# A row of silu(c) and a gate row leave the pool of load buffers: six shared places become four and two

## The chip, the cores and the metric

The kernel runs on one core of one Trainium2 chip. The time is device microseconds (us) of one execution. Before the change it was run three times: the median is 1897.98 us, the lowest 1897.97 and the highest 1900.49. One more execution was profiled; it took 1898.33 us, and its span, from the first to the last instruction in the trace, is 1896.6 us.

## What is computed

One residual block over 256 tokens of width 2048, in float32. Three sublayers follow each other, each with its own shift, scale and gate, which all come from one vector c:

```python
mod = (jax.nn.silu(c) @ w_ada[l] + b_ada[l]).reshape(B, N_SUBLAYERS, 3, D_MODEL)
shift, scale, gate = mod[:, :, 0], mod[:, :, 1], mod[:, :, 2]
y = _swiglu(modulate(x, 0), ffn1_w13[l], ffn1_w2[l])
x = _layer_norm(ALPHA * x + FFN_WEIGHT * gate[:, 0, None, :] * y, ln_g[l, 0], ln_b[l, 0])
u = modulate(x, 1)
...
y = jnp.concatenate([h_m, h_r], axis=-1) @ w_out[l]
x = _layer_norm(ALPHA * x + gate[:, 1, None, :] * y, ln_g[l, 1], ln_b[l, 1])
y = _swiglu(modulate(x, 2), ffn2_w13[l], ffn2_w2[l])
x = _layer_norm(ALPHA * x + FFN_WEIGHT * gate[:, 2, None, :] * y, ln_g[l, 2], ln_b[l, 2])
```

The first and the last sublayer are feed-forward networks (FFN) with an inner width of 5632; the middle one is the mixer, which runs four mLSTM heads beside a gated linear recurrence.

## The kernel before

**Weights.** All weights are read once, as tiles of 128x2048 floats (1 MB). Such a tile is loaded into a "raw" buffer by the SP queue (`load`, line 96, or `load_w`, line 115) and then split in two by `split` (line 103): ScalarE (ACT) rounds it into a "hi" tile (line 110) and VectorE (DVE) writes the rest into a "lo" tile (line 112). There are three hi and three lo buffers. The raw buffer is free again when the lo tile is written. TensorE (PE) then makes three products, hi by hi, lo by hi and hi by lo, so a tile in the FFNs is 24 matmuls of 512 columns.

**The raw pool.** `raw_tile` (line 84) hands out one of six equal places of 128x2048 floats (`RAW`, line 46). Not only weights live there. The row of silu(c), copied to all partitions (`scb`, line 171), takes one at the start and keeps it until its last reader. The gate of a sublayer (`gate`, line 191) takes another: `gate_rows` (line 224) writes the gate to HBM and reads it back to all partitions (line 233), and for the second and third sublayer it takes a new raw tile for that first (line 232). Beside these, rows of the layer norms (`ln_rows`, line 263), the recurrence's weights `wax` (line 1240) and the tile `sums` (line 690) pass through.

**The ada tiles.** The product of silu(c) with w_ada is made on DVE: 144 tiles are loaded into raw places, and each is multiplied with `scb` and summed by one instruction (line 209). `tick` (line 217) hands them out at a rate per load: 0.88 in the first FFN, 0.5 in the mixer and in the last FFN (lines 40 to 42). The last 16 of them, the third gate, fall into the first blocks of the last FFN.

**The last FFN.** After two ordinary blocks (`rows_block`, line 668), the blocks 2 to 9 are `fast_block` (line 710), which computes a 2x2 block product with seven products in place of eight. Of its loads, the tile `ta` (line 748) lives long: it is changed in place by subtractions at lines 755 and 760 and is read for the last time at line 774. `tc_` (line 752) is changed at line 765 and read until line 766, `td` (line 758) until 765. Each block has 12 loads: `ta`, `tc_`, `td`, `tb` (line 769), g2 and g3, two v tiles, and four of w2 (`x_tile`, line 732). Then follow a half block, `gate_rows` for the third gate, and `closing` (line 1025), which loads twelve w2 tiles, three of them multiplied with the gate (line 1034), and then the last layer norm's two rows.

**What sets the order.** Most instructions aren't ordered by hand. The framework orders the queue of each engine when the program is built (`schedule_with_timeline_sim`, line 1554): it goes through the instructions by their order in the code, with times of its own for each, and where the next one isn't ready in its reckoning (no place free, no data yet) it puts a later one first. On the chip each queue then runs in that fixed order. So a load is issued when it is at the head of SP's queue and its place is free, and an instruction on DVE or ACT that waits holds up all behind it. Instructions issued through `V`, `A`, `G`, `T` (line 140) keep the order of the code among themselves.

Of the kernel before, what the change touches and what calls it, by code (L numbers as in the profile page):

```python
# [11 lines left out]
F32 = mybir.dt.float32  # L12
# [4 lines left out]
P = 128  # L17
D = 2048
# [24 lines left out]

SLOT = 2176

RAW = 6

FAST = range(2, 10)


# [10 lines left out]
def block_kernel(ctx: ExitStack, tc: tile.TileContext, a: dict, out: bass.AP):  # L61
    nc = tc.nc
    cst = ctx.enter_context(tc.tile_pool(name="cst", bufs=1))
    big = ctx.enter_context(tc.tile_pool(name="big", bufs=1))
    wp = ctx.enter_context(tc.tile_pool(name="wp", bufs=1))
# [4 lines left out]
    def slot(name, dtype=F32):  # L70

        return ph.tile([P, SLOT], dtype, tag="slot", bufs=6, name=name)
# [5 lines left out]
    def bank(name):  # L78
        return psp.tile([P, 512], F32, tag="ps", name=name)
# [4 lines left out]
    def raw_tile(name):  # L84
        n_raw[0] += wide[0]
        if wide[0] and n_raw[0] % 3 == 0:
            return slot(name)[:, 0:D]
        return wp.tile([P, 2048], F32, tag="raw", bufs=RAW, name=name)


    credit = [0.0, 0.0]
# [1 line left out]

    fine = [False]

    def load(src, name, into=None):

        tick()
        raw = raw_tile("r" + name)
        queue().dma_start(raw, src)  # L100
        return raw, name, into

    def split(tile, act, low):

        raw, name, into = tile
        hi, lo = into() if into else [wp.tile([P, 2048], F32R, tag=w, bufs=3, name=w[0] + name) for w in ("hi", "lo")]
        step = 512 if fine[0] else 2048
        cols = [slice(c, c + step) for c in range(0, 2048, step)]
        for w in cols:
            act.copy(cut(hi, w), like(raw[:, w], hi))  # L110
        for w in cols:
            low.tensor_sub(cut(lo, w), like(raw[:, w], lo), cut(hi, w).bitcast(F32))  # L112
        return hi, lo

    def load_w(src, name, into=None):

        return split(load(src, name, into), nc.scalar, nc.vector)
# [24 lines left out]
    def queue():  # L142

        return Q if wide[0] else nc.sync
# [23 lines left out]
            T.matmul(ps[:, 0:P], ident, ident, start=True, stop=True)  # L168


    scb = raw_tile("scb")
    sc = cst.tile([P, KT], F32, name="sc")
    nc.scalar.dma_start(sc, a["c"])
    nc.scalar.activation(sc, sc, AF.Silu)
# [13 lines left out]
    badac = cst.tile([P, 3, 3, KT], F32, name="badac")  # L188
    adac = cst.tile([P, 3, 3, KT], F32, name="adac")
    modc = adac[:, :, 0:2, :]  # L190
    gate = Held(raw_tile("gate0"))
    dr = ctx.enter_context(tc.tile_pool(name="dr", bufs=1, space=bass.MemoryType.DRAM))
    rowd = dr.tile([KT, P], F32, name="rowd")
    xd = dr.tile([P, NT, D], F32, name="xd")
# [22 lines left out]
    def tick():  # L217

        credit[0] += credit[1]
        while todo and credit[0] >= 1.0:  # L220
            credit[0] -= 1.0
            ada_tile(V if wide[0] else nc.vector)

    def gate_rows(s, weight):

        ps = bank(f"adag{s}")
        nc.tensor.transpose(ps[0:KT, 0:P], adac[:, s, 2, :], ident)
        row = sm.tile([KT, P], F32, tag="grow", bufs=1, name=f"grow{s}")
        nc.scalar.mul(row, ps[0:KT, 0:P], weight)
        nc.gpsimd.dma_start(rowd, row)  # L230
        if s:
            gate.tile = raw_tile(f"gate{s}")
        nc.gpsimd.dma_start(gate[:, :], rowd.rearrange("a b -> (a b)").rearrange("(o n) -> o n", o=1).to_broadcast([P, D]))


# [48 lines left out]
    def mov_t(ps, hl, acth, actl, k0, t, first, last, pe=nc.tensor, **kw):  # L284

        hi, lo = hl
        tk = slice(t * P, (t + 1) * P)
        for j in range(4):
            w = slice(j * 512, (j + 1) * 512)
            o = like(ps, hi)  # L290
            pe.matmul(o, acth[:, k0 + j, tk], cut(hi, w), start=first and j == 0, stop=False, **kw)  # L291
            pe.matmul(o, acth[:, k0 + j, tk], cut(lo, w), start=False, stop=False, **kw)  # L292
            end = pe.matmul(o, actl[:, k0 + j, tk], cut(hi, w), start=False, stop=last and j == 3, **kw)  # L293
        return end
# [21 lines left out]
    def mov_w(pss, hl, acth, actl, k0, first, last, pe=nc.tensor):  # L316
        for t in range(NT):
            end = mov_t(pss[t], hl, acth, actl, k0, t, first, last, pe)
        return end
# [333 lines left out]
    def ffn(s, w13, w2, start, following=None):  # L653
# [11 lines left out]
        def new_h(gi):  # L665
            hts[gi] = [slot(f"{w}{gi}", F32R)[:, 0:GRP * S].rearrange("p (a b) -> p a b", a=GRP) for w in ("hth", "htl")]
# [43 lines left out]
        def fast_block(b, wh, wl):  # L710

            i = 8 * b
            gi = 4 * b // GRP - 1
            s2_, s4_, s3_, s1_ = 0, 4, 8, 12
            p1, p5 = bank(f"fa{b}"), bank(f"fb{b}")
            py = {}

            def part(ps, hl, h, k0, t, first, last):
                return mov_t(ps, hl, *h, k0, t, first, last, T, skip_group_check=not first and ps in (p1, p5))

            def fresh(k):
                return load(w13[i + k], f"fw{s}_{b}{k}")

            def halves(tile, w=""):
                return split((tile[0], tile[1] + w, None), nc.scalar, nc.vector)

            def kept(ps, tag, w):
                to = sm.tile([P, 512], F32, tag=tag, bufs=2, name=f"{w}{s}{b}")
                nc.scalar.copy(to, ps)
                return to  # L730

            def x_tile(m):
                n, k = b % 2 * 2 + m // 2, m % 2
                if not k:
                    py[n] = [bank(f"py{gi}_{n}_{t}") for t in range(NT)]
                kg = 2 * gi + k
                end = mov_w(py[n], load_w(w2[kg * 4 + n], f"w2{s}_{kg}_{n}"), *hts[gi], k * 4, not k, k == 1, T)
                if k:
                    c = slice(n * 512, (n + 1) * 512)
                    for t in range(NT):  # L740
                        if gi == 0:
                            evac.append(nc.scalar.copy(yacc[t][:, c], py[n][t]))
                        else:
                            nc.vector.tensor_add(yacc[t][:, c], yacc[t][:, c], py[n][t])
                return end

            u, w = (uh, ul), (wh, wl)
            ta = fresh(0)
            end = part(p1, halves(ta), u, 0, 0, True, True)
            turn_one(end)  # L750
            f1 = kept(p1, "u", "fs")
            tc_ = fresh(4)
            end = x_tile(0)
            turn_one(end)
            nc.vector.tensor_sub(ta[0], tc_[0], ta[0])
            part(p5, halves(ta, "p"), w, s1_, 0, True, True)
            f5 = kept(p5, "gy", "ft")
            td = fresh(5)
            x_tile(1)
            nc.vector.tensor_sub(ta[0], td[0], ta[0])  # L760
            part(p1, halves(ta, "q"), w, s2_, 0, False, True)
            f2 = kept(p1, "gy", "fv")
            part(p5, halves(td), w, s4_, 0, False, False)
            x_tile(2)
            nc.vector.tensor_sub(tc_[0], td[0], tc_[0])
            part(p1, halves(tc_, "q"), w, s3_, 0, False, True)
            f3 = kept(p1, "u", "fu")
            p2, p4 = bank(f"fc{b}"), bank(f"fd{b}")
            tb = fresh(1)
            part(p2, halves(tb), u, 4, 0, True, False)  # L770
            g2_ = load_w(w13[i + 2], f"fw{s}_{b}2")
            part(p2, g2_, u, 8, 0, False, False)
            part(p4, g2_, u, 8, 1, True, False)
            nc.vector.tensor_sub(tb[0], tb[0], ta[0])
            part(p4, halves(tb, "p"), u, 4, 1, False, False)
            g3_ = load_w(w13[i + 3], f"fw{s}_{b}3")
            part(p2, g3_, u, 12, 0, False, True)
            part(p4, g3_, u, 12, 1, False, True)
            nc.vector.tensor_add(f1, f1, p2)
            nc.scalar.activation(f1, f1, AF.Silu)  # L780
            nc.vector.tensor_add(f3, f3, p4)
            nc.scalar.activation(f3, f3, AF.Silu)
            x_tile(3)
            vs = [load_w(w13[i + 4 + k], f"fw{s}_{b}{4 + k}") for k in (2, 3)]
            for t, ps in enumerate((p5, p1)):
                for k in range(2):
                    part(ps, vs[k], u, 8 + 4 * k, t, False, k == 1)
            if 4 * b // GRP not in hts:
                new_h(4 * b // GRP)
            for t, h, v, ps in ((0, f1, f2, p5), (1, f3, f5, p1)):  # L790
                nc.vector.tensor_add(v, v, ps)
                nc.vector.tensor_mul(h, h, v)
                to_turn.append((b, t, h))
# [341 lines left out]
    def mixer(following):  # L1135
# [151 lines left out]
        rg_out()  # L1287
        ada_until(1, 2, KT - 1)
        gate_rows(1, 1.0)


# [266 lines left out]
```

## Time and profile before

| | value |
|---|---|
| median of three runs | 1897.98 us |
| profiled execution | 1898.33 us |
| its span | 1896.6 us |
| PE busy | 1864.0 us (98%) |
| DVE busy | 1562.4 us (82%) |
| ACT busy | 895.8 us (47%) |
| HBM read | 514.46 MB, 273 GB/s over the span |
| silu(c)'s row read last, from | 1377.3 us |
| stages, roughly | first FFN to 770 us, mixer to 1168, last FFN to the end |

The span is 1.7 us shorter than the profiled execution's time. PE stands for matmuls, and its busy time is the union of them; a matmul of 512 columns is listed with some 390 ns, but as they are pipelined one starts every 0.227 us when nothing is missing. "Idle before" in a row is the time for which the engine stood still ahead of it, with what ended the wait. SPq rows are the loads' issues.

### The profile page before, as it was taken

What the parts mean: (1) busy time and instruction counts of PE and PEld (TensorE: products, weight loads), DVE (VectorE), ACT (ScalarE), POOL (GpSimd) and SP (SyncE); (2) the same over time, 40 slices, a digit from 0 to 9 for tenths busy, and PEclk for the clock granted to TensorE, in tenths of its full rate; (3) what the DMA queues carried; (4) which work ended last, traced back from release to release, by engine and by line L of the source; (5) the groups of instructions that cost most, each with busy time, mean ns of one, the idle gap of its engine ahead of it and who ended that gap; (6) DMA issues with size and microseconds to landing.
All of it is one profiled execution on the core that took longest, in us unless ns stands there. A gap on an engine that the chain in (4) does not pass through costs nothing.

```text
span 1896.6 us, 21239 instructions
## 1 busy us (share of the span) xinstructions
PE 1864.0 (98%) x8495; PEld 1527.8 (81%) x8495; DVE 1562.4 (82%) x1467; ACT 895.8 (47%) x847; POOL 41.0 (2%) x68
## 2 busy tenths in 40 slices
PE   8999999999999999999699999999999999999998
PEld 5788888888888888788588887887788888888886
DVE  6899998887887977898976777798987788778776
ACT  4533444534333334756534346645555454555441
POOL 0000000000000000000000021000000000000000
PEclk9999999999999999999899999999999999999999
DMA  9999889989999886586487666758765654565661
GB/s 351 417 364 357 319 313 362 349 342 350 352 358 353 336 329 246 195 298 228 159 329 288 223 221 214 297 222 333 270 233 206 222 200 164 212 223 208 236 222 67
DMA packets 74931, 520.06 MB, mean 274 GB/s; under 512 B 8736, under 2 KB 8912, under 8 KB 13520
## 3 DMA queue, kind: packets, MB, share of 16 engines
q1 hardware_dynamic: 72144, 507.54, 71.0%
q0 software_dynamic: 960, 7.37, 1.0%
q10 hardware_dynamic: 1728, 3.80, 0.6%
q8 instruction: 66, 1.08, 0.2%
q14 instruction: 33, 0.27, 0.0%
HBM read 514.46 MB, written 4.22 MB: 273 GB/s over the span
## 4 chain that ended last, share of the span: by engine, by line
PE 92%; DVE 4%; ACT 2%; DMA 1%; issue 1%; POOL 0%; POOLq 0%; DVEq 0%; ACTq 0%
PE py L135 9%; PE pj L280 5%; PE fa L135 5%; PE fb L135 4%; PE fd L135 3%; PE fc L135 3%; PE py L292 3%; PE py L291 3%; PE py L293 3%; PE pj L282 3%; PE fg L292 3%; PE fg L293 3%; PE fg L291 3%; PE fv L293 2%; PE fv L291 2%; PE fv L292 2%
## 5 line engine op out<-in xcount | busy, mean ns | idle before, releaser
L209 DVE CUSTOM_DVE_ANT_0 ada<-ada,scb,badac 128x2048 f32<-128x2048 f32 x110 | 257.9, 2345 | 21.7 <-DMA ada<-in_w_ada 21.7
L110 ACT CAST hw<-rw 128x2048 fp32r<-128x2048 f32 x81 | 155.1, 1914 | 215.9 <-DMA rw<-in_w 51.0
L112 DVE TENSOR_TENSOR lw<-rw,hw 128x2048 fp32r<-128x2048 f32 x81 | 185.2, 2288 | 63.1 <-ACT hw L110 62.3
L112 DVE TENSOR_TENSOR lfw<-rfw,hfw 128x2048 fp32r<-128x2048 f32 x56 | 128.2, 2290 | 28.3 <-ACT hfw L110 28.1
L110 ACT CAST hfw<-rfw 128x2048 fp32r<-128x2048 f32 x56 | 107.3, 1915 | 58.6 <-PE py L135 28.2
L280 PE MATMUL pj<-u,hs 128*128 128x512 f32 x512 | 122.5, 391 | 0.0
L110 ACT CAST hra<-rra 128x2048 fp32r<-128x2048 f32 x38 | 72.6, 1914 | 101.7 <-DMA rra<-in_w_r 46.3
L280 PEld LDWEIGHTS pj<-u,hs 128*128 128x128 f32 x512 | 94.3, 188 | 18.4
L110 ACT CAST hs<-rs 128x2048 fp32r<-128x2048 f32 x32 | 61.1, 1909 | 83.9 <-PE pj L280 69.0
L135 PE MATMUL py<-lw,hth 128*128 128x512 f32 x256 | 99.7, 389 | 0.8 <-DVE lw L112 0.8
L135 PE MATMUL py<-hw,hth 128*128 128x512 f32 x256 | 100.4, 392 | 0.0
L292 PE MATMUL py<-lw,hth 128*128 128x512 f32 x256 | 99.9, 390 | 0.1
L135 PE MATMUL py<-hw,htl 128*128 128x512 f32 x256 | 99.7, 389 | 0.0
L293 PE MATMUL py<-hw,htl 128*128 128x512 f32 x256 | 99.7, 389 | 0.0
L291 PE MATMUL py<-hw,hth 128*128 128x512 f32 x256 | 97.3, 392 | 0.0
L110 ACT CAST hfg<-rfg 128x2048 fp32r<-128x2048 f32 x28 | 53.6, 1915 | 82.4 <-DMA rfg<-in_w 51.6
L112 DVE TENSOR_TENSOR lfv<-rfv,hfv 128x2048 fp32r<-128x2048 f32 x28 | 64.1, 2289 | 30.5 <-ACT hfv L110 30.2
L292 PE MATMUL fg<-lfg,u 128*128 128x512 f32 x224 | 87.4, 390 | 0.1
L293 PE MATMUL fg<-hfg,u 128*128 128x512 f32 x224 | 87.3, 390 | 0.0
L292 PE MATMUL fv<-lfv,u 128*128 128x512 f32 x224 | 87.2, 389 | 0.0
L293 PE MATMUL fv<-hfv,u 128*128 128x512 f32 x224 | 87.1, 389 | 0.0
L112 DVE TENSOR_TENSOR ls<-rs,hs 128x2048 fp32r<-128x2048 f32 x32 | 73.1, 2283 | 17.0 <-ACT hs L110 17.0
(723 smaller groups left out, 4733.1 us busy)
## 6 DMA issues: line engine op xcount, KB each, us to landing
ada<-in_w_ada SPq DMA_DIRECT2D x138, 1024.0 KB, 6.3
rw<-in_w SPq DMA_DIRECT2D x81, 1024.0 KB, 5.4
rfw<-in_w SPq DMA_DIRECT2D x64, 1024.0 KB, 4.8
rra<-in_w_r SPq DMA_DIRECT2D x45, 1024.0 KB, 7.0
rs<-in_w_s SPq DMA_DIRECT2D x32, 1024.0 KB, 5.0
rfg<-in_w SPq DMA_DIRECT2D x28, 1024.0 KB, 5.5
rfv<-in_w SPq DMA_DIRECT2D x28, 1024.0 KB, 5.1
rwo<-in_w_out SPq DMA_DIRECT2D x16, 1024.0 KB, 4.8
```

The lines of the kernel that those rows point to most:

```text
L110: act.copy(cut(hi, w), like(raw[:, w], hi))
L112: low.tensor_sub(cut(lo, w), like(raw[:, w], lo), cut(hi, w).bitcast(F32))
L135: self.last = getattr(self.engine, op)(*args, **kw)
L209: vec.tensor_tensor_reduce(raw[:, c], raw[:, c], scb[:, c], 1.0, base, ALU.mult, ALU.add, to)
L280: nc.tensor.matmul(ps, hi[:, k * P:(k + 1) * P], both(k), start=k == 0, stop=False)
L282: nc.tensor.matmul(ps[:, 0:S], lo[:, k * P:(k + 1) * P], uh[:, k, :], start=False, stop=k == KT - 1)
L291: pe.matmul(o, acth[:, k0 + j, tk], cut(hi, w), start=first and j == 0, stop=False, **kw)
L292: pe.matmul(o, acth[:, k0 + j, tk], cut(lo, w), start=False, stop=False, **kw)
L293: end = pe.matmul(o, actl[:, k0 + j, tk], cut(hi, w), start=False, stop=last and j == 3, **kw)
```

## The change

The pool of raw places shrinks from six to four. A second pool, tag "row", has two places of the same size. silu(c)'s row and the first gate go there; the second gate reuses the first one's tile; the third gate takes a row place anew. In the last FFN the tile `ta` of every fast block is loaded into a row place, and `tc_` too from block 4 on. The memory used in all is the same.

```diff
-RAW = 6
-
...
-        return wp.tile([P, 2048], F32, tag="raw", bufs=RAW, name=name)
+        return wp.tile([P, 2048], F32, tag="raw", bufs=4, name=name)
...
-    def load(src, name, into=None):
+    def load(src, name, into=None, raw=None):
 
         tick()
-        raw = raw_tile("r" + name)
+        raw = raw or raw_tile("r" + name)
         queue().dma_start(raw, src)
         return raw, name, into
...
-    scb = raw_tile("scb")
+    def row_tile(name):
+        return big.tile([P, D], F32, tag="row", bufs=2, name=name)
+
+    scb = row_tile("scb")
...
-    gate = Held(raw_tile("gate0"))
+    gate = Held(row_tile("gate0"))
...
-        if s:
-            gate.tile = raw_tile(f"gate{s}")
+        if s == 2:
+            gate.tile = row_tile("gate2")
...
-            def fresh(k):
-                return load(w13[i + k], f"fw{s}_{b}{k}")
+            def fresh(k, row=False):
+                return load(w13[i + k], f"fw{s}_{b}{k}", None, row_tile(f"fw{b}{k}") if row else None)
...
-            ta = fresh(0)
+            ta = fresh(0, True)
             end = part(p1, halves(ta), u, 0, 0, True, True)
             turn_one(end)
             f1 = kept(p1, "u", "fs")
-            tc_ = fresh(4)
+            tc_ = fresh(4, b >= 4)
```

## The prediction

> **What bounds the kernel now.** I read the page's span and busy times first, then the busy times by stage.
>
> ```profile
> span 1896.6 us, 21239 instructions
> ...
> PE 1864.0 (98%) x8495; PEld 1527.8 (81%) x8495; DVE 1562.4 (82%) x1467; ACT 895.8 (47%) x847; POOL 41.0 (2%) x68
> ```
>
> PE stands still for 1896.6 - 1864.0 = 32.6 us. The change removes no matmul, so it can move the time only through PE's idle time: by taking some of the 32.6 us away or by adding to it. The stages (window, its length, busy time of PE, PEld, DVE, ACT and POOL, PE clock, DMA share, GB/s) show where that time is:
>
> ```profile
> 300.00:700.00 400.00, 399.85 (x1784) 329.66 (x1783) 337.62 (x275) 162.44 (x111) 1.30 (x2) 1.00 0.92 351
> 770.00:882.00 112.00, 112.00 (x564) 92.32 (x563) 99.51 (x135) 66.58 (x85) 3.59 (x8) 1.00 0.71 258
> 882.00:940.00 58.00, 43.30 (x219) 36.42 (x218) 49.44 (x64) 41.08 (x62) 1.36 (x4) 0.88 0.37 131
> 940.00:1168.00 228.00, 228.00 (x1139) 192.58 (x1138) 172.45 (x231) 92.06 (x96) 20.00 (x26) 1.00 0.71 262
> 1168.00:1252.00 84.00, 83.63 (x372) 66.23 (x372) 69.16 (x81) 53.03 (x81) 3.08 (x5) 1.00 0.74 275
> 1252.00:1380.00 128.00, 125.01 (x555) 102.01 (x554) 117.48 (x75) 68.48 (x51) 0.00 (x0) 1.00 0.73 281
> 1380.00:1770.00 390.00, 390.00 (x1746) 322.83 (x1745) 307.58 (x190) 203.71 (x145) 2.21 (x4) 1.00 0.57 210
> 1770.00:1886.00 116.00, 116.00 (x521) 96.08 (x520) 86.23 (x91) 39.58 (x28) 1.68 (x2) 1.00 0.44 160
> ```
>
> The mixer's middle (882 to 940) holds 58.00 - 43.30 = 14.7 us of it, the first two fast blocks of the last FFN (1252 to 1380) 128.00 - 125.01 = 3.0 us, blocks 4 to 9 and the closing (1380 to 1886) none. The other 14.4 us lie in stretches that the change leaves as they are (up to 300, 700 to 770, after 1886) but for half a microsecond.
>
> **Where the places count changes.** I count places for loads, that is raw places without silu(c)'s row and the gate. The rows of those two (minimum, median and maximum duration in ns, first and last start) date the counts:
>
> ```profile
> L209 DVE CUSTOM_DVE_ANT_0 ada<-ada,scb,badac x110: 2332/2346/2353, 205.6 to 1377.3; 128x2048 f32<-128x2048 f32 x110
> ```
>
> ```profile
> L233 POOL DMA_DIRECT2D gate<-rowd x3: 557/560/570, 594.3 to 1757.8; - x3
> ...
> L135 PE MATMUL o<-gate,tot x2: 591/592/592, 763.6 to 764.0; 128*128 128x512 f32 x2
> ...
> L135 PE MATMUL f<-gate,tot x2: 591/592/592, 1168.1 to 1168.5; 128*128 128x512 f32 x2
> ```
>
> The first FFN has four places before and after: nothing to cost up to 764. From there until the second gate takes its tile (at the latest at its DMA, some time in 882 to 940) before has five, after has four. Then four and four until 1168. From 1168.5 before has five; after has four and one row place that only `ta` may use. From 1377.3 + 2.3 = 1379.7, when silu(c)'s row is read out, before has six; after four and two, the second for `tc_`. From the third gate (1757.8) before has five; after four, and one row place stands empty to the end.
>
> **764 to 882: five places become four.** What four places can do stands in the first FFN, with 0.88 ada tiles per load instead of the mixer's 0.5:
>
> ```profile
> ACT hfg L110 <- DMA rfg<-in_w: 51.6, 17, 4.5
> ACT hw L110 <- DMA rw<-in_w: 47.9, 14, 5.4
> ```
>
> These are waits in 300 to 700 (us in total, times, longest). The casts waited for transfers 31 times there in these two rows, for 99.5 us, and PE still was busy for 399.85 of 400 us: three split tiles ahead of it cover a late load. In the mixer's first half it is the other way round:
>
> ```profile
> ACT hs L110 <- PE pj L280: 26.1, 8, 3.7
> ...
> ACT hs L110 <- DMA rs<-in_w_s: 1.1, 1, 1.1
> ```
>
> Casts wait for PE to free a hi tile (8 times, 26.1 us), and for a transfer once. One place fewer delays a load by one release of a place; PE should not see it. Cost 0, hidden by the split tiles; without that cover each load would make PE wait for up to one release.
>
> The same step can shift an ada tile in DVE's order, and there the price is real, because DVE's chain ends PE's longest wait:
>
> ```profile
> 924.83 1.22 PE L291 MATMUL pv<-hv,u 128*128 128x512 f32 x2 [10.08 <-ACT hv L110]
> ```
>
> ```profile
> 921.81 1.17 ACT L1277 CAST rh<-t 128x512 fp32r<-128x512 f32 x2 [6.51 <-DVE t L1276]
> 922.88 1.89 ACT L110 CAST hv<-rv 128x2048 fp32r<-128x2048 f32 x1
> ```
>
> ```profile
> 884.09 0.33 SPq L100 DMA_DIRECT2D rv<-in_w_vo  x1
> ```
>
> ```profile
> rfw<-in_w SPq DMA_DIRECT2D x64, 1024.0 KB, 4.8
> ```
>
> PE waits 10.08 us for the cast of a tile whose load was issued at 884.09, 38.8 us before the cast. A transfer of 1 MB lands 4.8 us after its issue (the page's row, median), so no place is missing here: the cast stands in ACT's queue behind the recurrence's output, which waits for DVE. One ada tile more or fewer on DVE ahead of that moves the wait by its 2.35 us, either way. I take 0, since the count of places at 882 to 940 is four or nearly four in both, and keep -4.7 and +4.7 (two tiles) as bounds.
>
> **1168 to 1252.** Five become four and the reserved one. PE idles 0.37 us in 84, and at 0.5 ada tiles per load four places are asked for less than in 300 to 700. Cost 0.
>
> **Blocks 2 and 3, 1252 to 1380.** Here DVE is full (117.48 of 128 us), and before's five places are `ta`, `tc_`, `td`, a w2 tile and an ada tile. After has the same five while `ta` lives. The difference is between its last read and the next block:
>
> ```profile
> 1292.10 2.35 DVE L209 CUSTOM_DVE_ANT_0 ada<-ada,scb,badac 128x2048 f32<-128x2048 f32 x1 [1.51 <-DMA ada<-in_w_ada]
> ...
> 1294.38 2.29 DVE L774 TENSOR_TENSOR rfw<-rfw,rfw 128x2048 f32<-128x2048 f32 x1
> ```
>
> ```profile
> 1296.69 0.33 SPq L205 DMA_DIRECT2D ada<-in_w_ada  x1
> 1298.89 2.53 SPq L100 DMA_DIRECT2D rfw<-in_w  x2
> 1303.30 0.33 SPq L205 DMA_DIRECT2D ada<-in_w_ada  x1
> 1305.57 3.52 SPq L100 DMA_DIRECT2D rfw<-in_w  x2
> ```
>
> `ta`'s place is free at 1294.38 + 2.29 = 1296.67, and before an ada tile is issued into it at 1296.69; the next loads follow at 2.2 us steps, and the next block's `ta` is the first of the two at 1305.57. After, that `ta` is issued at 1296.7 instead, nine microseconds ahead of any need, and the four loads between come one step, 2.2 us, later; from 1305.57 on both stand alike. PE's longest wait in this stage says what that is worth:
>
> ```profile
> PE fc L135 <- DVE lfw L112: 1.5, 1, 1.5
> ```
>
> It is a wait for DVE, which was behind with its work; once, at 1292.10, it stood still 1.51 us for an ada tile. An early `ta` gives DVE nothing to do sooner, and a late ada tile costs only if DVE has nothing else in its order. Bounds: -3.0 us (all idle time of the stage goes) and +2.2 us in each of the two blocks, +4.4; I take 0, nearest to the casts of 300 to 700, which were late and not felt.
>
> **Block 4.** `tc_` must wait for silu(c)'s row to be read out, 1379.7. Its first reader comes late enough:
>
> ```profile
> 1388.14 2.29 DVE L755 TENSOR_TENSOR rfw<-rfw,rfw 128x2048 f32<-128x2048 f32 x1
> ```
>
> 1379.7 + 4.8 = 1384.5, ahead of 1388.14 by 3.6 us; other transfers in flight can eat that up, and I allow 2.3 us, one instruction of DVE, at the point where silu(c)'s last reader has just left DVE with less to do. Behind `tc_` on SP's queue stand block 4's other loads if the order puts it ahead of them. Cost 0, at most 2.3.
>
> **Blocks 4 to 9 and the closing.**
>
> ```profile
> 1738.73 2.29 DVE L774 TENSOR_TENSOR rfw<-rfw,rfw 128x2048 f32<-128x2048 f32 x1
> ...
> 1882.33 2.73 DVE L135 SCALAR_TENSOR_TENSOR x<-x,rsp,ln_b 128x512 f32<-128x512 f32 x4
> ```
>
> ```profile
> 1850.00 0.33 SPq L268 DMA_DIRECT2D ln_b<-in_ln_b  x1
> ```
>
> Six places become four and two for the very tiles that held two of the six. PE is busy for 390.00 of 390 us: nothing to gain; with a DMA share of 0.57 against the 0.92 at which four places sufficed, nothing to lose. The third gate needs a row place at 1757.8; block 9's `ta` has left it by 1738.73 + 2.29 = 1741.0. In the closing five become four; the last row, ln_b, is issued at 1850.00 and read at 1882.33, so even some releases later it is in time. Cost 0.
>
> **Sum**: 0 + 0 + 0 + 0 + 0 against the profiled execution's 1898.33 us (its span and 1.7 us around it), which is 0.35 us above the median; so 1897.98, rounded 1898.0.
>
> **The Trainium skill speaks against the change.** Its Perfetto Trace Analysis, section Identifying Performance Opportunities, says that the same gap repeating on the engine that should be saturated can mean that SBUF does not hold enough buffers for the next tile; by that rule fewer places give a bubble per block. The trace so far disagrees: with four places in 300 to 700 PE shows no bubble.
>
> **The rivals.**
> *Fewer places are felt (slower).* In blocks 2 and 3 the four loads after `ta`'s last read come 2.2 us late, the ada tile among them stands at the head of DVE's order, and DVE, full there, loses 2.2 us in each block: 1898.0 + 4.4 = 1902.4. It decides from DVE idle of 2 us ahead of line 209 in both blocks. For it speaks the 1.51 us wait at 1292.10; against it that DVE has other work. This is how the Trainium skill's rule would show here.
> *The mixer's chain comes later.* Two ada tiles more on DVE ahead of the scan: +4.7, 1902.7; one would stay at +2.35.
> *The mixer's chain comes earlier (faster).* Two ada tiles fewer: -4.7, 1893.3.
> *The last FFN's idle time goes.* The 3.0 us of blocks 2 and 3 vanish as `ta` no longer queues for a place: 1895.0.
> *The row places do nothing.* `ta` and `tc_` are just held elsewhere and all stays: 1898.0, which cannot be told from the forecast.
>
> **The numbers.** A measurement of this kernel can tell about 0.2% (3.8 us) from no change. Chances: forecast, with the idle row places, 0.45; places felt 0.15; chain later 0.13; chain earlier 0.15; idle time gone 0.12, of which 0.05 with an ada tile out of the mixer's chain besides (-5.35) and so over 0.2%. Faster 0.20, same 0.45 + 0.07 = 0.52, slower 0.28. The range goes from -3.0 - 2.35 = -5.35 (1892.6), which holds the earlier chain's -4.7 too, to +4.4 + 2.35 = +6.75 (1904.7): places felt and one ada tile more in the mixer. The forecast's own range is two microseconds either side.
>
> **What would show it.** Right: PE's idle time in 1252 to 1380 within 1 us of 3.0, `ta` issued right after line 774's end, no PE wait after 1380, and PE's wait for hv near 10 us. Wrong: that wait off by 2 us or more with another count of ada tiles between 770 and 921, or DVE waits at line 209 in blocks 2 and 3 of over 2 us each.

## The result and the profile after

The changed kernel takes 1882.22 us (median of 4 runs, 1881.04 to 1882.71), the kernel before in the same rounds 1898.92 us (4 runs, 1897.97 to 1900.49). The ratio is 0.991, 95% interval 0.9893 to 0.9928. The prediction was 1898.0 with a range from 1892.6; the result lies 10.4 us below that range. The profiled execution took 1882.46 us, 15.9 us less than the one of before.

From the page of the changed kernel, its span and busy times:

```profile
span 1880.7 us, 21240 instructions
...
PE 1861.4 (99%) x8495; PEld 1526.0 (81%) x8495; DVE 1561.3 (83%) x1467; ACT 895.1 (48%) x847; POOL 43.2 (2%) x68
```

PE's idle time fell from 32.6 to 1880.7 - 1861.4 = 19.3 us, by 13.3. The other 2.6 us are busy time: the same 8495 matmuls took 1864.0 us before and 1861.4 now. The stages, with the columns of the prediction's table (the mixer ends 20 us earlier now, so the windows from 1168 on hold somewhat later work than before):

```profile
770.00:882.00 112.00, 112.00 (x571) 92.59 (x570) 96.79 (x129) 65.04 (x79) 3.60 (x8) 1.00 0.70 252
882.00:940.00 58.00, 57.69 (x289) 49.08 (x288) 54.27 (x59) 43.13 (x61) 1.25 (x3) 1.00 0.68 256
...
1168.00:1252.00 84.00, 84.00 (x380) 69.57 (x379) 69.59 (x57) 44.06 (x44) 0.00 (x0) 1.00 0.71 266
1252.00:1380.00 128.00, 124.42 (x542) 100.90 (x540) 111.37 (x70) 67.42 (x52) 0.00 (x0) 0.99 0.74 280
1380.00:1770.00 390.00, 388.69 (x1737) 321.77 (x1737) 311.51 (x199) 201.32 (x142) 2.21 (x4) 1.00 0.56 205
```

The mixer's middle has no hole any more: 57.69 of 58 us busy where it was 43.30, at a clock of 1.00 where it was 0.88. The last FFN is a little worse: 124.42 of 128 (125.01), 388.69 of 390 (390.00).

For sums over stages I use two matmuls that both kernels have, one at the end of the first FFN (o from gate and tot) and one at the end of the mixer (f from gate and tot). Their rows in the changed kernel (minimum, median, maximum duration in ns; first and last start):

```profile
L133 PE MATMUL o<-gate,tot x2: 591/592/592, 760.6 to 761.1; 128*128 128x512 f32 x2
...
L133 PE MATMUL f<-gate,tot x2: 591/592/592, 1148.1 to 1148.6; 128*128 128x512 f32 x2
```

With before's 763.6 and 1168.1 and the spans, the three stages are: up to the first mark 763.6, now 760.6 (-3.0); from there to the second 404.5, now 387.5 (-17.0); from there to the end of the span 728.5, now 732.6 (+4.1). The sum is -15.9. PE's busy time in these three stages was 756.51, 389.17 and 718.29 us before and is 754.43, 386.56 and 720.45 now: 2.1 less, 2.6 less and 2.2 more. So three things happened, and each needs a cause.

**The mixer.** ACT's timeline in the changed kernel shows what moved (start, duration, what was done, and in brackets the idle time ahead of it):

```profile
903.38 1.91 ACT L108 CAST hv<-rv 128x2048 fp32r<-128x2048 f32 x1
...
935.00 0.62 ACT L1278 CAST rh<-t 128x512 fp32r<-128x512 f32 x1 [2.23 <-DVE t L1277]
```

Before, the first cast to hv stood at 922.88, behind the first rh at 921.81. Now it stands at 903.38 and rh comes 32 us after it. This tile was not loaded earlier: its load is issued at 884.93 (884.09 before).

```profile
884.93 0.33 SPq L98 DMA_DIRECT2D rv<-in_w_vo  x1
```

```profile
911.57 0.48 PE L292 MATMUL pv<-hv,u 128*128 128x512 f32 x1
```

PE starts the v product at 911.57 without a wait. For this tile ACT's order has changed, not the transfer. The whole stage lost 14.4 us of idle time and 2.6 us of busy time.

**The clock after the hole.** Windows of the kernel before, around the end of its wait (PE's busy time is the second number, the granted clock the third from the end):

```profile
924.83:929.00 4.17, 1.22 (x2) 0.50 (x2) 4.17 (x7) 1.23 (x2) 0.00 (x0) 0.50 0.00 0
929.00:933.00 4.00, 3.91 (x11) 3.10 (x12) 4.00 (x6) 0.00 (x0) 0.11 (x1) 0.59 0.69 246
933.00:940.00 7.00, 5.41 (x24) 4.05 (x23) 5.80 (x6) 6.56 (x5) 0.00 (x0) 1.00 0.55 190
```

After the 10.08 us without a matmul the granted clock was 0.50 and was back at 1.00 from 933. The Trainium skill, TensorE: Matmul & The Clock Gate, section What's actually happening, says that the array runs at half clock after an idle window of some 3.4 us, until it has been busy for as long. The trace agrees: 0.50 behind the wait. That fits the 2.6 us by which the mixer's matmuls got shorter (e1, with the kernel before's start and last FFN, has 386.66 us there); a stall of this length costs more than its idle time.

The other two stages show the same on a small scale, and nearly cancel. At the start of the kernel before, four matmuls behind a wait of 4.11 us took 3.38 us at a clock of 0.55. In the last FFN of the changed kernel a wait of only 2.58 us was followed by a clock of 0.50 (1264.60 to 1267.00). That is shorter than the Trainium skill's window, so in this case a wait need not fill it; the measurement decides.

**The last FFN.** PE's waits from 1180 to 1560 in the changed kernel (us in total, times, longest):

```profile
PE fa L133 <- DVE lfw_20q L110: 2.6, 1, 2.6
PE py L133 <- DVE lw L110: 2.1, 2, 1.3
PE th L814 <- DVE fu L793: 0.2, 1, 0.2
```

The first is in block 2, at a split of ta after its second subtraction, the longest of the second kind in block 4. The wait for fc of 1.5 us that before had is gone. Where the 4.1 us are lost shows beside e5 below, whose mixer ends at the same time: by matmuls to fb that both kernels have, the changed kernel is 2.2 us behind at the end of block 2 (1300.17 against 1297.99), still 2.2 at block 3, and 4.0 from block 4 on (1387.15 against 1383.14).

### The profile page after: what moved, and what is told of

It reads as the page before. It is cut to its first block, busy times and chain, and to the rows that moved or that the text cites. A ratio compares the mean times of both kernels' runs of the same rounds, so it can differ in the third digit from the quotient of the medians.

```text
span 1880.7 us, 21240 instructions
## 1 busy us (share of the span) xinstructions
PE 1861.4 (99%) x8495; PEld 1526.0 (81%) x8495; DVE 1561.3 (83%) x1467; ACT 895.1 (48%) x847; POOL 43.2 (2%) x68
## 4 chain that ended last, share of the span: by engine, by line
PE 92%; DVE 4%; DMA 2%; issue 1%; ACT 1%; POOL 0%; POOLq 0%; DVEq 0%; SPq 0%; ACTq 0%
PE py L133 9%; PE pj L281 5%; PE fa L133 5%; PE fb L133 4%; PE fc L133 3%; PE fd L133 3%; PE py L293 3%; PE py L294 3%; PE py L292 3%; PE pj L283 3%; PE fg L293 3%; PE fg L294 3%; PE fg L292 3%; PE fv L293 3%; PE fv L292 3%; PE fv L294 3%
## 5 line engine op out<-in xcount | busy, mean ns | idle before, releaser
L110 DVE TENSOR_TENSOR lfw<-rfw,hfw 128x2048 fp32r<-128x2048 f32 x48 | 109.9, 2289 | 17.2 <-ACT hfw L108 17.2
L108 ACT CAST hfw<-rfw 128x2048 fp32r<-128x2048 f32 x48 | 91.9, 1915 | 47.8 <-PE py L133 28.2
L294 PE MATMUL fg<-hfg,u 128*128 128x512 f32 x224 | 87.3, 390 | 0.0
L108 ACT CAST hfv<-rfv 128x2048 fp32r<-128x2048 f32 x28 | 53.6, 1913 | 66.7 <-DMA rfv<-in_w 41.3
L292 PE MATMUL fg<-hfg,u 128*128 128x512 f32 x224 | 84.5, 392 | 0.0
```

## The experiments

**The theories.** What the builder reckoned is not on record; what is said of it here is inferred from the code and from the order that came out. The builder gives out the places of a pool in the order of the code. In the kernel before, the second gate takes a shared place, and its line stands ahead of the loads of the v tiles. Its place is taken only when the gate's DMA is placed, and that needs the last ada column of the gate, a transpose and a copy. T1: the builder therefore put the v loads behind the gate's DMA in its reckoning, and so their casts behind rh in ACT's fixed order; on the chip the load came early, but the cast kept its turn. The change takes the second gate out of this queue. R1, the rival: the number of places up to 882 (five, now four) shifted the order. R0: the row places in the last FFN bring the time. T2, for the start: before 50 us the first gate's place was not in use yet, so before had five places there and not the four that I counted. T3, for the last FFN: places that are short there, in three forms below. T4: tc_ of block 4 waits for silu(c)'s row.

All lengths below are from profiled executions, by the two marks above; the last two columns are from the timed runs. The interval is that of the ratio to the kernel before in the same rounds, whose median there was between 1898.88 and 1899.60. One profiled execution per kernel gives the lengths, and it can lie off the median: by -1.7 us in e1, -2.0 in e9 and +1.0 in e10.

| kernel | start | mixer | last FFN | median us | ratio, 95% interval |
|---|---|---|---|---|---|
| before | 763.6 | 404.5 | 728.5 | 1898.92 | 1 |
| changed | 760.6 | 387.5 | 732.6 | 1882.22 | 0.9893 to 0.9928 |
| e1 gate reused | 762.7 | 387.6 | 728.5 | 1882.34 | 0.9900 to 0.9927 |
| e2 gate later | 764.5 | 387.2 | 728.4 | 1881.55 | 0.9892 to 0.9920 |
| e3 gate raw again | 760.4 | 404.9 | 734.7 | 1901.27 | 1.0001 to 1.0018 |
| e4 gate0 early | 760.5 | 404.5 | 728.4 | 1895.54 | 0.9976 to 0.9994 |
| e5 e1 and e4 | 760.5 | 387.5 | 728.5 | 1878.34 | 0.9882 to 0.9912 |
| e6 ta reserved | 760.7 | 387.6 | 730.0 | 1880.23 | 0.9888 to 0.9915 |
| e7 tc_ from block 5 | 760.7 | 387.5 | 734.1 | 1884.79 | 0.9914 to 0.9939 |
| e8 changed again | 760.5 | 387.5 | 732.9 | 1882.71 | 0.9900 to 0.9927 |
| e9 ada later | 760.6 | 387.6 | 729.4 | 1881.29 | 0.9893 to 0.9920 |
| e10 ta's row from 3 | 760.5 | 387.5 | 740.9 | 1889.81 | 0.9936 to 0.9961 |
| e11 row used | 760.5 | 387.5 | 730.8 | 1880.68 | 0.9886 to 0.9916 |
| e12 e11 and e7 | 760.5 | 387.5 | 730.1 | 1880.13 | 0.9880 to 0.9913 |

### e1: the kernel before, the second gate reuses the first one's tile

```diff
-        if s:
+        if s == 2:
             gate.tile = raw_tile(f"gate{s}")
```

> The kernel before, in which only one thing is changed: the second gate keeps the first gate's tile instead of taking a new shared place. Theory T1: in the built order the second gate's place stands ahead of the places of the v tiles, and is taken only when its DMA is placed, behind the last ada column and the gate's transpose; so the loads of the v tiles and with them their casts come late in ACT's order. With the tile reused the wait for hv goes: the mixer is 17.3 us shorter, start and last FFN stay as before, 1898.9 - 17.3 = 1881.6 us. Rival R0, that the row places in the last FFN bring the time: 1898.9, no change. Rival R1, that four places in place of five between 764 and 882 us bring it, gives 1881.6 here too, since there are four here as well; the next two kernels tell T1 and R1 apart.

1882.34 us. The mixer is 387.6 long as in the changed kernel, start and last FFN are within a microsecond of before. This one edit brings the whole gain of the mixer; the new pool is not needed for it, and R0 falls.

### e2: the kernel before, the second gate later in the code

```diff
-        gate_rows(1, 1.0)
         v = slot("v")...
         for n in range(2):
...
+        gate_rows(1, 1.0)
         kt_ = v8(slot("k"))
```

> The kernel before, in which the second gate still takes a shared place of its own, but the call stands behind the loop over the v tiles in the code instead of ahead of it; six places as before, so five for loads in the mixer's first half. T1 (the place's turn in the code holds up the v loads): the wait for hv goes, about 17.3 us less, 1881.6 us, within 3 us as the order differs in small things. R1 (it is the number of places): the stall stays, 1898.9 us.

1881.55 us, mixer 387.2. The number of places is that of before, five up to the gate, and the second gate still takes its own. ACT's order is the short one:

```profile
907.06 1.91 ACT L110 CAST hv<-rv 128x2048 fp32r<-128x2048 f32 x1
```

R1 falls: it isn't the number.

### e3: the changed kernel, the second gate back in the shared pool

```diff
+        if s == 1:
+            gate.tile = raw_tile("gate1")
         if s == 2:
             gate.tile = row_tile("gate2")
```

> The changed kernel, in which the second gate takes one of the four shared places again, at the same place in the code as in the kernel before; all else as changed. T1: the wait for hv is back, PE waits some 10 us at the first matmul of the v product and the clock goes down behind it, 1882.2 + 17.3 = 1899.5 us, or more, as only three places are left for loads until 1168 us. R1: the number of places up to 882 us is four as in the changed kernel, so the stall stays away, 1882.2 us.

1901.27 us, mixer 404.9. PE's and ACT's rows are those of before again:

```profile
922.24 1.22 PE L294 MATMUL pv<-hv,u 128*128 128x512 f32 x2 [10.65 <-ACT hv L108]
```

```profile
919.22 1.17 ACT L1280 CAST rh<-t 128x512 fp32r<-128x512 f32 x2 [6.86 <-DVE t L1279]
920.29 1.89 ACT L108 CAST hv<-rv 128x2048 fp32r<-128x2048 f32 x1
```

With four places up to 882 the stall is back. With e1 and e2 this is shown from both sides: a new place for the second gate, taken at that turn in the code, makes the stall. ACT's order follows as T1 says: the first cast to hv starts ahead of the first rh in e1 (905.5 and 937.1) and e2 (907.1 and 941.5) and behind it in e3 (920.3 and 919.2). Why the builder's reckoning gives that order stays inferred. Three places for loads from the gate on did the mixer no further harm (404.9 against 404.5).

### e4: the kernel before, the first gate's place held from the start

```diff
     gate = Held(raw_tile("gate0"))
+    nc.gpsimd.memset(gate[:, 0:1], 0.0)
```

> The kernel before, with one small memset on POOL that writes the first column of the first gate's tile at the start, so that this tile holds its place from the start as in the changed kernel. Theory T2: before 50 us the gate's place served the loads, the fifth ada tile was loaded ahead of the fourth one and of the second weight tile and delayed both; with the place held the two go first and PE is 3.3 us earlier from 36 us on: 1898.9 - 3.3 = 1895.6 us, the mixer's stall as before. Rival: the start's gain comes from silu(c)'s row standing in another pool; then this does nothing, 1898.9 us.

1895.54 us; the start is 760.5 as in the changed kernel, the rest as before. SP's queue of the kernel before and of e4 from 8 us on (start, time over all of the group, what is loaded):

```profile
8.30 6.74 SPq L205 DMA_DIRECT2D ada<-in_w_ada  x6
15.46 2.20 SPq L882 DMA_DIRECT2D rra<-in_w_r  x2
```

```profile
8.21 4.18 SPq L206 DMA_DIRECT2D ada<-in_w_ada  x4
13.34 1.63 SPq L883 DMA_DIRECT2D rra<-in_w_r  x2
15.44 4.70 SPq L206 DMA_DIRECT2D ada<-in_w_ada  x4
```

Six halves of ada tiles stood ahead of the weight tile rra, now four: with one place fewer the fifth ada tile can't go first, the rest comes 2 us earlier, and PE's wait for u falls from 4.1 us to 2.3 in two waits. The clock does the rest: in e4 it stays at 1.00 from 20 to 36 us, and PE's busy time up to the first mark is 754.55 us where it was 756.51. T2 is shown: a place less made the start faster, because the place too many was filled with something that nobody needed yet. The row that dates the place is the first write to the gate's tile in the kernel before; the tile serves for partial sums long before it holds the gate:

```profile
L135 ACT COPY gate<-rg x2: 575/582/588, 50.4 to 50.8; 128x512 f32<-128x512 f32 x2
```

### e5: e1 and e4 together

> The kernel before with the two edits that gave the gains when made alone: the second gate keeps the first one's tile, and the first gate's tile holds its place from the start. Six shared places, no row pool; the last FFN is that of the kernel before. If the two gains are independent and the change's own last FFN is the part that gives time back: 1898.9 - 17.3 - 3.3 = 1878.3 us, some 4 us below the changed kernel, with the stage from 1168 us on as long as in the kernel before. Rival: what the changed kernel loses in the last FFN comes from the earlier end of the mixer (other phase of the loads), then this loses it too, 1882.

1878.34 us, the number expected, and the two gains add: 760.5, 387.5 and 728.5. Its last FFN is that of before, though it starts 20 us earlier; so what the changed kernel loses there is its own doing and no matter of phase. It has the lowest median of the study: by the stages 4.1 us better than the changed kernel, all of it in the last FFN.

### e6: e5 with one shared place kept for ta

```diff
...
-            ta = fresh(0)
+            ta = load(w13[i], f"fw{s}_{b}0", None, kept_ta)
...
+            kept_ta = raw_tile("kept_ta")
             for b in FAST:
```

> The kernel with both edits, in which one of the six shared places is taken ahead of block 2 and kept for ta of all fast blocks; nothing else goes to a place of its own. Theory T3: after ta's last read its place stands empty until the next block's ta, the ada tile that used it in the kernel before waits for another place, and as it stands ahead of the lo tile of ta (q) in DVE's order, PE waits for that tile in block 2: the wait for fa of some 2.6 us (4.4 us of lost time) is back and the wait for fc of 1.5 us is gone, block 4 loses nothing as tc_ takes any place: 1878.3 + 2.1 = 1880.4 us. Rival: the loss in the changed kernel comes from tc_'s place alone (block 4), then this is as the kernel with both edits, 1878.3 us, and no wait for fa is seen.

1880.23 us. The total is right and the mechanism isn't: there is no wait for fa. PE's waits from 1180 to 1560:

```profile
PE fc L135 <- DVE lfw L112: 1.2, 1, 1.2
PE py L135 <- DVE lw L112: 1.1, 2, 0.8
PE th L814 <- DVE fu L793: 0.7, 1, 0.7
PE th L814 <- DVE sg L800: 0.5, 1, 0.5
PE fb L135 <- DVE lfw L112: 0.4, 1, 0.4
```

The last FFN is 1.5 us longer than in e5 (one profiled execution each; the timed runs of the two overlap). Keeping a place empty between two ta, which was my rival's mechanism in the prediction, costs about that much and not the 4.1, and at another spot: block 2 ends no later than in e5 (1297.77 against 1297.99), the loss lies in blocks 3 and 4. In e6 that place is taken in its turn, and the load of block 2's ta is issued at 1219.72; in the changed kernel the row place is free from the end of the mixer, and this ta goes there at once:

```profile
L98 SPq DMA_DIRECT2D fw<-in_w x1: 328/328/328, 1150.2 to 1150.2; - x1
L108 ACT CAST hfw<-fw x1: 1912/1912/1912, 1232.2 to 1232.2; 128x2048 fp32r<-128x2048 f32 x1
```

It is issued at 1150.2 and first read at 1232.2, 82 us later. All that time the fifth place is full of a tile that nobody needs, and blocks 0 and 1 live on four.

### e7: the changed kernel, tc_ in a row place from block 5 on

```diff
-            tc_ = fresh(4, b >= 4)
+            tc_ = fresh(4, b >= 5)
```

> The changed kernel, in which tc_ of block 4 comes from the four shared places and takes the row place from block 5 on only. Theory T4: in block 4 tc_ waits for the last reader of silu(c)'s row, DVE waits 3.1 us for its data ahead of the subtraction and PE loses 1.7 us at the first w2 tile of that block; here that goes, 1882.2 - 1.7 = 1880.5 us, seen in the profile as no wait ahead of that subtraction. Rival: the shared places are short in block 4 as well, something else of the four comes late in its place, 1882.2 us or more.

In the changed kernel the last reader of silu(c)'s row ends at 1363.46 + 2.35 = 1365.81, and tc_ of block 4 is issued at 1365.85, into its place:

```profile
1363.46 2.35 DVE L210 CUSTOM_DVE_ANT_0 ada<-ada,scb,badac 128x2048 f32<-128x2048 f32 x1 [2.17 <-DMA ada<-in_w_ada]
...
1373.49 2.29 DVE L756 TENSOR_TENSOR fw<-fw,fw 128x2048 f32<-128x2048 f32 x1 [3.10 <-DMA fw<-in_w]
```

```profile
1365.85 0.33 SPq L98 DMA_DIRECT2D fw<-in_w  x1
1366.22 2.15 SPq L98 DMA_DIRECT2D rw<-in_w  x2
```

It took 7.6 us, with two other tiles behind it, and DVE stood still for 3.10. In e7 that wait is gone, and between matmuls on both sides of it (1320.03 and 1386.79 in the changed kernel) PE took 1.8 us less (1.3 less than in e8, the changed kernel again). That part of T4 is shown. The total was not: 1884.79 us. PE's waits in e7:

```profile
PE fa L133 <- DVE lfw_20q L110: 3.8, 1, 3.8
PE py L133 <- DVE lw L110: 1.9, 2, 1.1
PE th L814 <- DVE fu L793: 0.7, 1, 0.7
```

The wait in block 2, where e7 has the changed kernel's order, was 3.8 us instead of 2.6, and block 3 lost more as well. The difference shows first in block 1, at one ada tile; DVE's rows in the changed kernel, in e8 (the same kernel again) and in e7:

```profile
1211.12 2.35 DVE L210 CUSTOM_DVE_ANT_0 ada<-ada,scb,badac 128x2048 f32<-128x2048 f32 x1 [2.90 <-DMA ada<-in_w_ada]
```

```profile
1211.97 2.35 DVE L210 CUSTOM_DVE_ANT_0 ada<-ada,scb,badac 128x2048 f32<-128x2048 f32 x1 [3.83 <-DMA ada<-in_w_ada]
```

```profile
1212.79 2.35 DVE L210 CUSTOM_DVE_ANT_0 ada<-ada,scb,badac 128x2048 f32<-128x2048 f32 x1 [4.31 <-DMA ada<-in_w_ada]
```

The wait for fa was 2.6, 3.5 and 3.8 us in these three. In these profiles what DVE stands still longer here, 50 us earlier, comes out at PE nearly in full. That pointed to blocks 0 and 1.

### e8: the changed kernel again

> The changed kernel once more, unchanged, on the same chip and in the same rounds as the two kernels below. The kernel with tc_ of block 4 in a shared place came out at 1884.8 us where T4 expected 1880.5, though its order is that of the changed kernel up to block 4 and its wait in block 4 is gone; if the level of the chip or of the moment does that, the changed kernel lies at about 1884 to 1887 us here; if not, at 1882.2 again, and then T4's total is wrong.

1882.71 us, as at first. The kernel before was at its usual level beside e7 too (1899.60 us, 9 runs). But e7 has the changed kernel's order ahead of block 4, so moving tc_ can hardly be what slowed blocks 1 to 3 there. And e3, whose last FFN is written as in the changed kernel, lost as much: 734.7 us, with a wait for fa of 3.9 us. Why one transfer took longer, and why all five runs of e7 lie above those of e8, stays open; only the gain of 1.3 to 1.8 us in block 4 is settled.

### e9: the changed kernel, the ada tiles one load later

```diff
+            credit[0] -= 0.5
             for b in FAST:
```

> The changed kernel, in which the ada tiles of the last FFN are handed out one load later from block 2 on (half a credit less); in the built order the ada tile that stood ahead of the lo tile of ta (q) in block 2 then stands behind it. Theory T3b: what costs the 4.4 us in block 2 is that place in DVE's order, not the number of places: the wait for fa goes, PE is some 3.6 us earlier behind block 2 than in the changed kernel. In block 4 tc_ has to wait for silu(c)'s row one load longer, which may give back up to 5 us there. Rival T3a (four shared places are too few for blocks 2 and 3): a wait of the same size stays in block 2 at another tile.

The wait for fa is gone, and a matmul behind block 2 (fb, 1267.16 in the changed kernel) starts 4.2 us earlier. PE's waits from 1180 to 1560:

```profile
PE fa L133 <- DVE lfw_30q L110: 1.8, 1, 1.8
PE fa L133 <- DVE lfw_40q L110: 0.9, 1, 0.9
PE fb L133 <- DVE lfw_40p L110: 0.8, 1, 0.8
```

So moving one ada tile behind the split that PE waits for is enough in block 2, but a part comes back as waits of the same kind in blocks 3 and 4. The median, 1881.29 us, can't be told from the changed kernel's; the 729.4 us in the table are from the fastest of four runs.

### e10: the changed kernel, ta of block 2 in the shared places

```diff
-            ta = fresh(0, True)
+            ta = fresh(0, b >= 3)
```

> The changed kernel, in which ta of block 2 comes from the four shared places and only the ta of blocks 3 to 9 from the row place; so block 2 has four places in all where the changed kernel has four and one. T3a (number of places): block 2 loses more than in the changed kernel, over 4.4 us. T3b (order): in the built order the ada tile stands behind the lo tile of ta (q) here too, the wait of 2.6 us for that tile goes, and block 2 loses less than in the changed kernel, about 1 us; the total is then 2 to 4 us below the changed kernel of the same rounds.

1889.81 us: T3b's number is wrong, and the loss is over 4.4 us as T3a says. The wait for that split did go, as the order said, but PE waited 6.0 us for a cast and 3.8 for lo tiles instead:

```profile
PE py L133 <- ACT hw L108: 6.0, 1, 6.0
PE py L133 <- DVE lw L110: 3.8, 4, 1.5
```

With four places for all in block 2, the last FFN loses 740.9 - 728.5 = 12.4 us where the changed kernel loses 4.1 (this profile is of the slowest of five runs; the median is 7.6 us above the changed kernel's). By e9 and e10 the order decides which wait shows, and the number of places how much is lost.

### e11: the changed kernel, block 1 uses the row place

```diff
...
+                    row = row_tile(f"fg{b}{k}") if s == 2 and k % 2 == 0 else None
+                    hl = split(load(w13[i + k], f"fg{s}_{b}{k}", None, row), nc.scalar, nc.vector)
...
+                    row = row_tile(f"fv{b}{k}") if s == 2 and k % 2 == 0 else None
+                    hl = split(load(w13[i + 4 + k], f"fv{s}_{b}{k}", None, row), nc.scalar, nc.vector)
...
```

> The changed kernel, in which every second tile of the last FFN's second ordinary block (four of its eight) is loaded into the row place that stands with ta of block 2 in it there, loaded 82 us ahead of its first use; so block 1 has four and one places for loads instead of four, and the ada tile stays ahead of the lo tile of ta (q) in DVE's order. Theory T3c: DVE falls behind in blocks 0 and 1 already, because with four places its ada tiles land late (idle time ahead of the ada tiles of 11.8 us in 92 us, 5.1 us with five places), and PE pays for it at the first wait where DVE has no lead left, fa in block 2. Then that idle time falls to some 5 to 7 us here, the wait for fa to under 1 us, and the total is 1882.5 - 3.6 = 1879 us. T3b (only the order of the ada tile in block 2 counts): the wait for fa stays at 2.6 to 3.5 us, 1882.5 us.

1880.68 us. The idle time of DVE ahead of the ada tiles between 1170 and 1262 (last number of the row), in the changed kernel, e5 and e11:

```profile
L210 DVE CUSTOM_DVE_ANT_0 ada<-ada,scb,badac 128x2048 f32<-128x2048 f32 x7 | 16.4, 2350 | 11.8 <-DMA ada<-in_w_ada 11.7
```

```profile
L210 DVE CUSTOM_DVE_ANT_0 ada<-ada,scb,badac 128x2048 f32<-128x2048 f32 x7 | 16.4, 2349 | 5.1 <-DMA ada<-in_w_ada 4.9
```

```profile
L210 DVE CUSTOM_DVE_ANT_0 ada<-ada,scb,badac 128x2048 f32<-128x2048 f32 x7 | 16.4, 2348 | 3.6 <-DMA ada<-in_w_ada 3.6
```

It fell from 11.8 to 3.6 (12.8 in e8, 13.8 in e7), and no wait for lfw_20q is left although the ada tile still stands ahead of it:

```profile
1255.89 2.35 DVE L210 CUSTOM_DVE_ANT_0 ada<-ada,scb,badac 128x2048 f32<-128x2048 f32 x1 [1.59 <-DMA ada<-in_w_ada]
```

T3c is shown for block 2: blocks 0 and 1 were short of a place, and block 2 paid; now it ends at 1297.39, no later than in e5. The total is 1.7 us above the one expected; in blocks 3 and 4 PE waits for lo tiles of w2 again (2.3 us in three waits from 1180 to 1560).

### e12: e11 with tc_ from block 5 on

> The kernel of the run before with tc_ of block 4 in a shared place besides. T3c and T4 together: the wait for fa is gone and the 1.4 to 1.7 us in block 4 too, 1882.5 - 3.6 - 1.6 = 1877.3 us, no slower than the kernel before with the two edits (1878.3 us). If the shared places are short in block 4: no better than the run before.

1880.13 us. Block 4's wait is gone here too, but the stage is only 0.7 us shorter than e11's and 1.6 longer than e5's. The shared pool of six, e5, keeps the lower median (1878.34 us), though single runs of the two overlap.

## Why the prediction was wrong

**What bounds the kernel.** Right that only PE's holes can move, and that 14.7 us of them lie in 882 to 940. Incomplete in one point: the matmuls behind the hole ran at a clock of 0.50, so in the mixer 2.6 us more were to be had than the idle time.

**"The first FFN has four places before and after: nothing to cost up to 764."** Wrong up to 50 us. I dated the gate's place by its DMA at 594 and by the code line that makes the tile; the tile is first written at 50.4 us, and until then loads used the place. Worth -3.0 us (e4).

**764 to 882, and the wait for hv.** This is the step that failed. I wrote that "no place is missing here: the cast stands in ACT's queue behind the recurrence's output, which waits for DVE", and stopped there. The first half is true on the chip. What I didn't ask is what had put the cast behind the recurrence's output, when its data was there some 34 us earlier (issued at 884.09, 4.8 us to land, cast at 922.88). I took ACT's order as given and priced the wait by DVE's chain, at 2.35 us for an ada tile. The chain did move: the group rows for 770 to 924, before and now, have 7 and 10 ada tiles, and the first rh comes at 935.00 instead of 921.81.

```profile
L209 DVE CUSTOM_DVE_ANT_0 ada<-ada,scb,badac 128x2048 f32<-128x2048 f32 x7 | 16.4, 2341 | 2.8 <-DMA ada<-in_w_ada 2.8
```

```profile
L210 DVE CUSTOM_DVE_ANT_0 ada<-ada,scb,badac 128x2048 f32<-128x2048 f32 x10 | 23.4, 2339 | 0.5 <-DMA ada<-in_w_ada 0.5
```

By my rule that is some 7 us lost (the rival "chain later", in full), and it cost nothing, because PE no longer waits for anything behind it. The diff had one line that takes the second gate out of the shared pool; I read it as a matter of how many places there are, and never as one of whose turn comes when. Worth -17.0 us (e1, e2, e3). The cost of the place less was near 0 as predicted: the mixer takes 387.2 us with five places (e2) and 387.6 with four (e1). The sign that I gave for being wrong, the wait off by 2 us or more with another count of ada tiles, came true only by the letter: three tiles more go with a wait that is gone.

**1168 to 1252, "cost 0".** Wrong, and hidden in that stage itself: PE is busy for 84.00 of 84 us there. DVE lost its lead in it (e11), and PE paid in the next stage. I had put the "reserved" place beside four shared ones as if it could serve in these blocks; it held a tile loaded 82 us ahead of its use. The argument from 300 to 700, where casts were late and not felt, doesn't carry over: DVE has 338 of 400 us to do there and 117 of 128 in blocks 2 and 3.

**Blocks 2 and 3.** "I take 0" was wrong. The rival with +4.4 was near in size only by chance: the last FFN lost 4.1, of which 2.2 us in block 2 come from blocks 0 and 1 (e11) and the rest from block 4. Its mechanism (ta's empty place between two blocks) made 1.5 us in e6, and in blocks 3 and 4. The sign that PE's idle time in 1252 to 1380 stays within 1 us of 3.0 came out, at 3.6, by chance too: the waits behind it are others. The Trainium skill, Perfetto Trace Analysis, section Identifying Performance Opportunities, says that the same gap repeating on the engine that should be saturated can mean that there is no room for the next tile. The runs agree in part: fewer places gave PE waits of 6.0 and 3.8 us in e10, but as single long waits, most of them in block 2, and not as one gap that repeats in every block.

**Block 4.** The reason was named (silu(c)'s row, then the transfer) and the bound of 2.3 us held, with 1.3 to 1.8 lost (e7; 1.0 by e12 against e11). The value taken, 0, was wrong: the transfer took 7.6 us and not 4.8, as I had feared it might.

**Blocks 5 to 9 and the closing.** Right: PE is busy for 388.69 of 390 us from 1380, and block 4's wait of 1.3 us is what is missing.

The sum as it came out is -3.0 - 17.0 + 4.1 = -15.9 us; the prediction had 0 + 0 + 0.

## What to carry to other kernels

When an instruction runs long after its data is there, ask what fixed its place in its engine's queue: where a builder hands out the places of a pool in the order of the code, a tile that gets its data late can hold back what belongs to later loads of that pool, in the built order if not on the chip. (It need not: at the start the first gate's place served loads until its first write.) So read a change of a pool for turns as well as for numbers, and date a place by its tile's first write, not by the line that names it. A reserved place that is filled long ahead of its use is a place less for all others, and the engine that loses its lead by it shows the loss one stage later, where the bound engine first waits for it.

## What the runs showed that was not expected

More places can be slower: at the start a fifth place let a tile go first that nobody needed, and PE lost 3 us (e4), 2.0 of them because the matmuls behind its wait ran slower. The same ada transfer in the same order let DVE wait 2.90, 3.83 and 4.31 us in three profiled executions, and with four places the difference reached PE nearly undamped; the runs don't show what makes it. A wait of 2.58 us was enough for the granted clock to go to 0.50, while after waits of 1.8 us (at the start of the changed kernel and in block 3 of e9) it stayed at 1.00.
